# The gate operands of a PEER layer laid out by pairs of tokens

## The chip, the cores and the metric

The kernel runs on one core of a Trainium2 chip. The metric is the device time of one execution in microseconds, taken as the median of several runs. An engine is one of TensorE (matmuls, in the profile PE, its weight loads PEld), VectorE (DVE), ScalarE (ACT), GpSimd (POOL) and the queues that issue DMAs, SP's and POOL's here.

## The reference, cut to what matters

One inference step of a two-layer decoder for 512 prompt tokens and 8 single sample tokens, model width 1024. Each layer ends with a PEER block, a mixture of 16384 tiny experts. For every token and each of 8 heads it picks 16 experts, 128 in all, by two top-16 searches over 128 keys each; an expert's index is `i * 128 + j` of the two keys found. A gate `g` is the softmax of the 16 scores of a head.

```python
eidx = ...                       # (T, 8, 16): 128 * i + j
g = jax.nn.softmax(top_s, axis=-1)
u = u_tab[eidx]; vv = v_tab[eidx]
act = jax.nn.gelu(jnp.einsum('thkd,td->thk', u, h))
return jnp.einsum('thk,thkd->td', g * act, vv)
```

Written densely, the block is `y[t] = sum over i, j of G[t, i, j] * gelu(u[i, j] . h[t]) * v[i, j]`, where `G[t, i, j]` is the gate of expert (i, j) for token t, and zero for an expert that t did not pick.

## The kernel before, in words

Two of the four tiles of 128 prompt tokens in a layer are computed by gathering each token's experts: one indirect DMA on POOL and one pass over 1024 elements on VectorE for each of the rows of `u` and of `v` (`peer_tile`, lines 708 to 721). The other two tiles, 256 tokens, are computed densely in `dense_peer`, the function around the change. The gathers of a layer run beside its dense part; a planner puts VectorE's instructions on gathered rows between the dense ones, tied to marks that the dense code leaves (`tick`, line 104).

The dense part goes over the first key index i in 4 groups q of `QI` = 32. For a group there are three kinds of work:
- `acts(q)` (line 478): for each of the 32 values of i, a tile of `u` for 128 experts comes by DMA, is multiplied with the 256 tokens on TensorE (`ps_a`, 8 matmuls of 256 columns in group 0 and 24 in the others), and ScalarE writes `gelu` of it into `W[q]`, laid out (j, i, token).
- `gates(q)` (line 502): multiplies `W[q]` by the gates. This is what the change touches.
- the `y` matmuls (lines 570 to 574): for each i, `W[q][:, i]` times a tile of `v`, four matmuls of 512 columns (12 in most of the last group), added up in four PSUM banks over all 128 values of i.

While the `y` matmuls of group q run, the loop (lines 550 to 584) steps `acts(q + 1)` in the first 4 values of i and `gates(q + 1)` in the other 28. `acts(1)` is stepped beside `gates(0)`.

`gates(q)` makes the 128 by 32 matrix of gates of each token with two matmuls. Partition p of the operands is one of the token's 128 picks. The weights are a one-hot of the pick's j (128 columns, `oh[:, :, k]`); the moving operand is a one-hot of its i within the group times its gate (32 columns, `gi[:, c, :, t - t0]`), once for each of two 16-bit parts c of the gate, which are added in PSUM. The 32 result columns go to `ps[:, :, t - t1]`, a PSUM tile laid out (i, 16 tokens), so they are 64 bytes apart there; VectorE multiplies that tile into `W[q]` (line 537).

Two operands feed it:
- `gi`, for 32 tokens at a time: VectorE compares `sq`, the picks' i less 32 q, with `iotaJ`, a table of 128 values with each one standing 8 times (line 509), and multiplies the result by either part of the gate (line 514). Before the change `gi` is laid out (part, i, token): the 32 columns of a token are 32 elements of 2 bytes, 64 bytes, apart. The comparison runs over rows of 8 tokens.
- `oh`, for 8 tokens at a time, four buffers: VectorE compares in one instruction (line 521), and then the 128 columns of one token are 16 bytes apart; or ScalarE builds it with eight instructions and one over all (lines 527 and 530), and then they lie one behind the other. The choice (line 520) gives VectorE half of group 0 in both layers, and half of groups 1 to 3 in layer 1; all the rest is ScalarE's. There are 4 x 256 x 2 x 2 = 4096 gate matmuls and 256 one-hot operands.

The sample tokens have a PEER path of their own; in its top-16 pick, line 443 multiplies 256 elements of 2 bytes, of which one operand is read in rows of a single element (for the prompt tiles, in rows of 8).

The order of instructions on each engine is set by a planner from priorities and estimated durations.

Of the kernel before, what the change touches and what calls it, by code (L numbers as in the profile page):

```python
# [11 lines left out]
HF = mybir.dt.float16  # L12
# [3 lines left out]
OP = mybir.AluOpType  # L16
# [19 lines left out]
def body(ctx: ExitStack, tc: tile.TileContext, a):  # L36
    nc = tc.nc
    V, SC, PE, GP, SY = nc.vector, nc.scalar, nc.tensor, nc.gpsimd, nc.sync
# [27 lines left out]
    iotaJ = per.tile([128, 128, 8], HF, name="iotaJ")  # L66
# [37 lines left out]
    def tick(ins, k=1):  # L104
        if cur[0] is not None:
            anchors[cur[0]].extend([ins.ins.name] * k)
# [362 lines left out]
    def dense_peer(layer, dpa, open_rest, open_odd, smp):  # L469
# [3 lines left out]
        NQ, QI, NV = 4, 32, 4  # L473
# [28 lines left out]
        def gates(q):  # L502

            selJ, selb = dd["sel"]
            sq = dpb.tile([128, 256], HF, name="selq", tag="selq", bufs=1)
            V.tensor_scalar(sq, selb[:, 0, :], float(-q * QI), None, op0=OP.add)
            for t0 in range(0, 256, 32):
                gi = dpb.tile([128, 2, QI, 32], HF, name="gi", tag="gi", bufs=2)
                V.tensor_tensor(gi[:, 1].rearrange("p i (m w) -> p i m w", w=8),
                                sq[:, None, t0:t0 + 32].rearrange("p i (m w) -> p i m w", w=8)  # L510
                                .to_broadcast([128, QI, 4, 8]),
                                iotaJ[:, :QI, None, :].to_broadcast([128, QI, 4, 8]), op=OP.is_equal)
                for k in range(2):
                    V.tensor_tensor(gi[:, k], gi[:, 1], selb[:, 2 + k, None, t0:t0 + 32].to_broadcast([128, QI, 32]),  # L514
                                    op=OP.mult)
                for t1 in range(t0, t0 + 32, 16):
                    ps = pt.tile([128, QI, 16], F32, name="ps_g", tag="tr")
                    for t2 in range(t1, t1 + 16, 8):
                        oh = dpb.tile([128, 128, 8], HF, name="ohj", tag="ohj", bufs=4)
                        if (t2 // 8) % 4 < ([2, 2][layer] if not q else 2 * J_DVE[layer][q]):  # L520
                            V.tensor_tensor(oh, selb[:, 1, None, t2:t2 + 8].to_broadcast([128, 128, 8]), iotaJ,
                                            op=OP.is_equal)
                        else:

                            oh = oh.rearrange("p j k -> p (j k)").rearrange("p (k j) -> p j k", k=8)
                            for k in range(8):
                                SC.activation(oh[:, :, k], iota128, AF.Abs, scale=-1.0,  # L527
                                              bias=selJ[:, t2 + k:t2 + k + 1])
                            oh2 = oh.rearrange("p j k -> p k j")
                            SC.activation(oh2, oh2, AF.Relu, bias=1.0, scale=-1.0)  # L530
                        for k in range(8):
                            t = t2 + k
                            for c in range(2):
                                PE.matmul(ps[:, :, t - t1], oh[:, :, k], gi[:, c, :, t - t0], start=c == 0,  # L534
                                          stop=c == 1)
                    wv = W[q][:, :, t1:t1 + 16]
                    tick(V.tensor_tensor(wv, ps, wv, op=OP.mult), [3, 1][layer] if q else [5, 3][layer])  # L537
                    yield
# [4 lines left out]
        dpb, py = open_rest()  # L543
# [3 lines left out]
        for _ in gates(0):  # L547
            for _ in range(2):
                next(na, None)
        for q in range(NQ):  # L550
            na, ng = (na if not q else acts(q + 1), gates(q + 1)) if q + 1 < NQ else (iter(()), iter(()))
            for il in range(QI):
                i = q * QI + il
                w = W[q][:, il, :]
# [649 lines left out]
```

## Time and profile before

| | us |
|---|---|
| median of 3 runs | 3308.31 |
| lowest and highest | 3303.71, 3317.15 |
| the profiled execution | 3307.97 |
| its span, first to last instruction | 3306.3 |
| TensorE matmuls busy | 3051.4 |
| VectorE busy | 2426.3 |
| ScalarE busy | 1380.7 |
| GpSimd busy | 1340.0 |
| gate matmuls (line 534) busy | 265.5 in 4096 |
| gate weight loads (line 534) busy | 250.3 in 4096 |
| y matmuls (line 574) busy | 701.8 in 1536 |
| gate operands (lines 509 and 514) busy | 43.5 in 64, 87.4 in 128 |

Busy time counts every moment once, so matmuls that overlap in the pipeline add up to less than their number times their mean. Layer 0's gates run from 735 to 1518 us, layer 1's from 2444 to 3187 us.

### The profile page before, as it was taken

The page shows a single profiled execution, that of the slowest core. Times are in us where ns is not written, and L with a number is a line of the kernel's source. Part 1 is how long each engine was busy: PE and PEld are TensorE (multiplying, and loading weights), DVE is VectorE, ACT ScalarE, POOL GpSimd, SP SyncE. Part 2 cuts the span into 40 slices and gives each one's busy share as a digit, 9 for nine tenths or more (in the row PEclk, how much of TensorE's full clock was granted, in tenths as well). Part 3 has the DMA queues.
Part 4 walks back from the last instruction along what each step waited for, and adds up shares of the span by engine and source line. Part 5 has one row for each costly group of instructions (what it writes and reads, how often), then busy time and mean ns, then how long its engine had stood idle before and what let it go on. Part 6 is the DMA issues. An engine that isn't in the chain of part 4 may idle for free.

```text
span 3306.3 us, 50069 instructions
## 1 busy us (share of the span) xinstructions
PE 3051.4 (92%) x18048; PEld 2304.3 (70%) x18048; DVE 2426.3 (73%) x5093; ACT 1380.7 (42%) x3154; POOL 1340.0 (41%) x1061
## 2 busy tenths in 40 slices
PE   7998979859999999999998998789799999999999
PEld 7898646759757866866887643455689658768757
DVE  1489789999876668676425689869978776786775
ACT  2344021216666277386453234321246443353534
POOL 0046663564554436441000556534234454344340
PEclk9999989879999999999999988799899999999999
DMA  7788987888998989985655989867778999889885
GB/s 253 228 287 307 338 311 272 317 313 293 345 356 322 353 306 357 359 318 184 206 168 174 366 315 344 287 243 276 268 264 285 343 352 359 319 300 359 308 293 165
DMA packets 271563, 976.54 MB, mean 295 GB/s; under 512 B 30938, under 2 KB 31770, under 8 KB 271306
## 3 DMA queue, kind: packets, MB, share of 16 engines
q0 software_dynamic: 152064, 553.72, 46.5%
q1 hardware_dynamic: 119250, 419.62, 36.2%
q8 instruction: 142, 2.33, 0.3%
q14 instruction: 107, 0.88, 0.1%
HBM read 966.76 MB, written 6.46 MB: 294 GB/s over the span
## 4 chain that ended last, share of the span: by engine, by line
PE 66%; DVE 13%; DMA 9%; issue 5%; ACT 4%; POOL 3%; SPq 0%; DVEq 0%; POOLq 0%; ACTq 0%
PE y L574 19%; PE ps_d L231 7%; PE ps_g L534 7%; PE ps_a L488 6%; PE ps_a L489 5%; PE ps_a L491 5%; PE ps_a L494 3%; DMA gath<-peer_u,ix 3%; DMA gath<-peer_v,ix 3%; POOL gath L704 3%; DVE gath L713 2%; DVE x L720 2%; PE y L570 2%; PE y L571 2%; PE y L572 2%
## 5 line engine op out<-in xcount | busy, mean ns | idle before, releaser
L704 POOL DMA_INDIRECT gath<-peer_u,ix x512 | 649.0, 1268 | 1098.0 <-DVE ix L672 491.9
L704 POOL DMA_INDIRECT gath<-peer_v,ix x512 | 652.2, 1274 | 715.0 <-DVE x L720 383.9
L574 PE MATMUL y<-vb,W 128*128 128x512 f32 x1536 | 701.8, 602 | 1.2 <-DVE W L537 0.9
L720 DVE SCALAR_TENSOR_TENSOR x<-gath,act,x 128x1024 f32<-128x1024 f32 x512 | 655.5, 1280 | 64.4 <-DMA gath<-peer_v,ix 58.6
L713 DVE SCALAR_TENSOR_TENSOR gath<-gath,h_g 128x1024 f32<-128x1024 f32 x512 | 615.0, 1219 | 87.4 <-DMA gath<-peer_u,ix 83.6
L527 ACT ACTIVATE ohj<-iota,selJ 128x128 f16<-128x128 f32 x1408 | 425.8, 388 | 219.0 <-PE ps_g L534 205.7
L574 PEld LDWEIGHTS y<-vb,W 128*128 128x128 f32 x1536 | 282.7, 193 | 297.7 <-issue 293.7
L231 PE MATMUL ps_d<-hT,wt 128*128 128x128 f32 (+3 forms) x2048 | 430.7, 368 | 25.3 <-DMA wt<-peer_wq 5.8
L488 PE MATMUL ps_a<-hPh,wh 128*128 128x256 f32 x1536 | 403.7, 299 | 12.6 <-ACT wh L209 12.6
L231 PEld LDWEIGHTS ps_d<-hT,wt 128*128 128x128 f32 x2048 | 303.9, 198 | 137.8 <-issue 17.0
L489 PE MATMUL ps_a<-hPl,wh 128*128 128x256 f32 x1536 | 385.0, 287 | 0.0
L211 DVE TENSOR_TENSOR wl<-ub,wh 128x1024 fp32r<-128x1024 f32 x192 | 234.6, 1223 | 175.4 <-ACT wh L209 136.8
L209 ACT ACTIVATE wh<-ub 128x1024 fp32r<-128x1024 f32 x192 | 202.2, 1054 | 299.8 <-PE ps_a L489 251.6
L488 PEld LDWEIGHTS ps_a<-hPh,wh 128*128 128x128 f32 x1536 | 300.4, 196 | 26.5 <-ACT wh L209 14.6
L489 PEld LDWEIGHTS ps_a<-hPl,wh 128*128 128x128 f32 x1536 | 300.2, 195 | 10.1 <-issue 10.1
L534 PEld LDWEIGHTS <-ohj 128*128 128x128 f16 x4096 | 250.3, 130 | 72.1 <-issue 48.4
L534 PE MATMUL ps_g<-gi,ohj 128*128 128x32 f16 x4096 | 265.5, 234 | 18.9 <-DVE gi L514 11.6
L494 PE MATMUL ps_a<-hT,ub 128*128 128x256 f32 x1024 | 233.8, 390 | 31.4 <-ACT W L499 31.4
L494 PEld LDWEIGHTS ps_a<-hT,ub 128*128 128x128 f32 x1024 | 199.9, 197 | 61.8 <-ACT W L499 32.2
L499 ACT ACTIVATE W<-ps_a 128x256 f32<-128x256 f32 x256 | 96.2, 379 | 339.2 <-PE ps_a L491 149.3
L491 PE MATMUL ps_a<-hPh,wl 128*128 128x256 f32 x1536 | 225.1, 290 | 1.6 <-DVE wl L211 1.6
L491 PEld LDWEIGHTS ps_a<-hPh,wl 128*128 128x128 f32 x1536 | 200.2, 193 | 11.2 <-issue 8.4
(298 smaller groups left out, 3815.7 us busy)
## 6 DMA issues: line engine op xcount, KB each, us to landing
ub<-peer_ut SPq DMA_DIRECT2D x256, 512.0 KB
vb<-peer_v SPq DMA_DIRECT2D x256, 512.0 KB
wt<-w_in SPq DMA_DIRECT2D x64, 512.0 KB
wt<-peer_wq SPq DMA_DIRECT2D x64, 512.0 KB
wt<-w_out SPq DMA_DIRECT2D x32, 512.0 KB
gath<-peer_u,ix POOLq DMA_INDIRECT x512
gath<-peer_v,ix POOLq DMA_INDIRECT x512
wt<-w_k SPq DMA_DIRECT2D x16, 512.0 KB
```

Of the source, the lines that this page charges most:

```text
L211: tick(V.tensor_tensor(wl, w, wh.bitcast(F32), op=OP.subtract), k)
L231: z = PE.matmul(ps[:, :n], wt[:, c, :], rhs[:, c0 + c, :n], start=c0 + c == 0, stop=c0 + c == nk - 1)
L488: PE.matmul(ps, uh[:, c, :], hP[0][:, c, :], start=c == 0, stop=False)
L489: PE.matmul(ps, uh[:, c, :], hP[1][:, c, :], start=False, stop=False)
L491: PE.matmul(ps, ul[:, c, :], hP[0][:, c, :], start=False, stop=c == 7)
L494: z = PE.matmul(ps, u[:, c, :], hT[:, c, :256], start=c == 0, stop=c == 7)
L527: SC.activation(oh[:, :, k], iota128, AF.Abs, scale=-1.0, bias=selJ[:, t2 + k:t2 + k + 1])
L534: PE.matmul(ps[:, :, t - t1], oh[:, :, k], gi[:, c, :, t - t0], start=c == 0, stop=c == 1)
L574: PE.matmul(y[t][hf], w[:, ts], v[:, hs], start=i == 0, stop=i == 127)
L704: GP.indirect_dma_start(out=t, out_offset=None, in_=table, in_offset=bass.IndirectOffsetOnAxis(ap=ix[:, k:k + 1], axis=0))
L713: z = V.scalar_tensor_tensor(u, u, 1.0, h, op0=OP.mult, op1=OP.mult, accum_out=act[:, k:k + 1])
L720: z = V.scalar_tensor_tensor(x[t], v, act[:, k:k + 1], x[t], op0=OP.mult, op1=OP.add)
```

## The change

`gi` is laid out (part, pair of tokens, i, token of the pair) in place of (part, i, token). The 32 columns of one token's moving operand are then 2 elements, 4 bytes, apart, and the two tokens of a pair lie side by side. The three VectorE instructions that fill it for 32 tokens go over the same 1024 elements in that order, and read the three sources through one view each: pairs of tokens, each pair repeated for the 32 values of i. `iotaJ` is read two of its eight equal elements at a time. Everything else stays.

```diff
--- before.py
+++ after.py
@@ -505,14 +505,13 @@
             sq = dpb.tile([128, 256], HF, name="selq", tag="selq", bufs=1)
             V.tensor_scalar(sq, selb[:, 0, :], float(-q * QI), None, op0=OP.add)
             for t0 in range(0, 256, 32):
-                gi = dpb.tile([128, 2, QI, 32], HF, name="gi", tag="gi", bufs=2)
-                V.tensor_tensor(gi[:, 1].rearrange("p i (m w) -> p i m w", w=8),
-                                sq[:, None, t0:t0 + 32].rearrange("p i (m w) -> p i m w", w=8)
-                                .to_broadcast([128, QI, 4, 8]),
-                                iotaJ[:, :QI, None, :].to_broadcast([128, QI, 4, 8]), op=OP.is_equal)
+
+                gi = dpb.tile([128, 2, 16, QI, 2], HF, name="gi", tag="gi", bufs=2)
+                sv = [z[:, t0:t0 + 32].rearrange("p (m w) -> p m w", w=2)[:, :, None, :].to_broadcast([128, 16, QI, 2])
+                      for z in (sq, selb[:, 2], selb[:, 3])]
+                V.tensor_tensor(gi[:, 1], sv[0], iotaJ[:, None, :QI, :2].to_broadcast([128, 16, QI, 2]), op=OP.is_equal)
                 for k in range(2):
-                    V.tensor_tensor(gi[:, k], gi[:, 1], selb[:, 2 + k, None, t0:t0 + 32].to_broadcast([128, QI, 32]),
-                                    op=OP.mult)
+                    V.tensor_tensor(gi[:, k], gi[:, 1], sv[1 + k], op=OP.mult)
                 for t1 in range(t0, t0 + 32, 16):
                     ps = pt.tile([128, QI, 16], F32, name="ps_g", tag="tr")
                     for t2 in range(t1, t1 + 16, 8):
@@ -531,7 +530,7 @@
                         for k in range(8):
                             t = t2 + k
                             for c in range(2):
-                                PE.matmul(ps[:, :, t - t1], oh[:, :, k], gi[:, c, :, t - t0], start=c == 0,
+                                PE.matmul(ps[:, :, t - t1], oh[:, :, k], gi[:, c, (t - t0) // 2, :, t % 2], start=c == 0,
                                           stop=c == 1)
                     wv = W[q][:, :, t1:t1 + 16]
                     tick(V.tensor_tensor(wv, ps, wv, op=OP.mult), [3, 1][layer] if q else [5, 3][layer])
```

## Rows read from the trace of the kernel before

**Rows 1.** The page: busy time by engine; the chain that ended last, by line.
```profile
PE 3051.4 (92%) x18048; PEld 2304.3 (70%) x18048; DVE 2426.3 (73%) x5093; ACT 1380.7 (42%) x3154; POOL 1340.0 (41%) x1061
...
PE y L574 19%; PE ps_d L231 7%; PE ps_g L534 7%; PE ps_a L488 6%; PE ps_a L489 5%; PE ps_a L491 5%; PE ps_a L494 3%; DMA gath<-peer_u,ix 3%; DMA gath<-peer_v,ix 3%; POOL gath L704 3%; DVE gath L713 2%; DVE x L720 2%; PE y L570 2%; PE y L571 2%; PE y L572 2%
```

**Rows 2.** Busy time by engine in seven stretches; columns named by their first line.
```profile
core 0: us, PE busy (x) PEld busy (x) DVE busy (x) ACT busy (x) POOL busy (x), PEclk, DMA share, GB/s
735.00:875.00 140.00, 130.49 (x1253) 125.81 (x1254) 127.65 (x171) 93.37 (x211) 72.92 (x52) 0.95 0.87 303
890.00:1040.00 150.00, 149.64 (x839) 85.71 (x840) 99.81 (x158) 103.66 (x282) 78.60 (x68) 0.95 0.94 353
1182.00:1289.00 107.00, 104.69 (x717) 64.81 (x715) 79.13 (x113) 100.74 (x280) 53.16 (x44) 0.98 0.87 312
1418.00:1519.00 101.00, 95.46 (x674) 57.90 (x673) 72.32 (x99) 95.70 (x260) 43.88 (x35) 0.97 0.81 289
2444.00:2578.00 134.00, 128.49 (x1243) 123.38 (x1243) 113.90 (x144) 89.54 (x198) 53.72 (x38) 0.96 0.75 261
2594.00:2738.00 144.00, 143.02 (x816) 82.43 (x816) 109.52 (x176) 50.55 (x140) 79.46 (x68) 0.99 0.96 357
2875.00:2962.00 87.00, 87.00 (x647) 54.98 (x646) 71.81 (x105) 50.36 (x135) 39.73 (x31) 1.00 0.85 295
```

**Rows 3.** Instructions on one-hot operands: duration ns min/median/max, first and last start.
```profile
L534 PE MATMUL ps_g<-gi,ohj x4096: 216/234/272, 735.1 to 3186.6; 128*128 128x32 f16 x196
...
L527 ACT ACTIVATE ohj<-iota,selJ x1408: 383/387/404, 710.6 to 3176.2; 128x128 f16<-128x128 f32 x176
...
L521 DVE TENSOR_TENSOR ohj<-selb,iotaJ x80: 670/683/694, 729.5 to 3168.3; 128x1024 f16<-128x1024 f16 x80
```

**Rows 4.** TensorE in order of time from 1249.85 us: start, duration, instruction, count.
```profile
1249.85 3.80 PE L534 MATMUL ps_g<-gi,ohj 128*128 128x32 f16 x64
```

**Rows 5.** TensorE in order of time, 1281.35 to 1284.77 us, granted clock 0.50.
```profile
1281.52 1.08 PE L534 MATMUL ps_g<-gi,ohj 128*128 128x32 f16 x16 [2.22 <-ACT ohj L530]
...
1283.19 0.41 PE L489 MATMUL ps_a<-hPl,wh 128*128 128x256 f32 x1
...
1283.41 0.41 PE L488 MATMUL ps_a<-hPh,wh 128*128 128x256 f32 x1
```

**Rows 6.** TensorE in order of time from 2872.3 us, granted clock 1.00.
```profile
2872.12 0.28 PE L488 MATMUL ps_a<-hPh,wh 128*128 128x256 f32 x1
2872.24 0.28 PE L489 MATMUL ps_a<-hPl,wh 128*128 128x256 f32 x1
```

**Rows 7.** TensorE from 1249.85 us, cut after two and after three gate matmuls.
```profile
1249.85 0.27 PE L534 MATMUL ps_g<-gi,ohj 128*128 128x32 f16 x2
...
1249.85 0.33 PE L534 MATMUL ps_g<-gi,ohj 128*128 128x32 f16 x3
```

**Rows 8.** Weight loads ahead of a near and a far row; 29 far matmuls.
```profile
1249.42 0.10 PEld L534 LDWEIGHTS <-ohj 128*128 128x128 f16 x1 [0.24 <-issue]
...
2885.17 0.14 PEld L534 LDWEIGHTS <-ohj 128*128 128x128 f16 x1 [0.24 <-issue]
...
2885.59 1.91 PE L534 MATMUL ps_g<-gi,ohj 128*128 128x32 f16 x29
```

**Rows 9.** Waits, 1182 to 1289 us: us in total, times, longest.
```profile
ACT ohj L527 <- PE ps_g L534: 6.3, 4, 3.3
...
PEld L534 <- ACT ohj L530: 3.8, 5, 2.4
...
PE ps_g L534 <- ACT ohj L530: 2.2, 1, 2.2
```

**Rows 10.** Groups by line and shape: count, busy us, mean ns, idle before.
```profile
L509 DVE TENSOR_TENSOR gi<-selq,iotaJ 128x1024 f16<-128x1024 f16 x64 | 43.5, 681 | 0.0
...
L514 DVE TENSOR_TENSOR gi<-gi,selb 128x1024 f16<-128x1024 f16 x128 | 87.4, 685 | 0.6
...
L211 DVE TENSOR_TENSOR wl<-ub,wh 128x1024 fp32r<-128x1024 f32 x192 | 234.6, 1223 | 175.4 <-ACT wh L209 136.8 <-issue 25.8 <-ACT W L499 4.8
...
L446 DVE TENSOR_TENSOR oh<-oh 128x256 f16<-128x256 f16 x16 | 4.5, 282 | 0.2
```

**Rows 11.** VectorE in order of time from 2422 us, the sample tokens.
```profile
2422.49 0.41 DVE L443 TENSOR_TENSOR oh<-oh,tmp 64x256 f16<-64x256 f16 x1
```

## The prediction

> **What bounds the kernel now.** I read the page first, then the stretches in which gate matmuls run, then single matmuls. On the page TensorE is busy 92% of the span and the gate matmuls stand on the chain that ended last with 7% of it, some 231 us of 3306.3 [rows 1]: the reader is to see that there is time of this line to win, and that it is not the largest line. The second view cuts out the stretches in which gates run, one for each of four groups of 32 rows of W in each of two layers [rows 2]. The reader is to look at which engine fills a stretch. In groups 1 and 2 of layer 1 (the last two rows; group 3, from 3102 us on, is like group 2) TensorE is busy 143.0 of 144 and 87.0 of 87 us while ScalarE has 51 and 50: TensorE alone sets the pace. Group 1 of layer 0 (second row) is alike, 149.6 of 150 with ScalarE at 103.7. In groups 2 and 3 of layer 0 ScalarE, which builds all one-hot operands there, is busy 100.7 of 107 and 95.7 of 101 us, about as much as TensorE. In the two groups 0 the chain changes hands: TensorE 130.5 of 140 and 128.5 of 134, VectorE 127.7 and 113.9.
>
> The third view counts the work [rows 3]: 4096 gate matmuls, each with its own weight load of 128 columns. Of the 256 one-hot operands, each serving 16 matmuls, ScalarE builds 1408 / 8 = 176 with their 128 weight columns lying one behind the other (2816 matmuls, "near" below) and VectorE 80 with weight columns 16 bytes apart (1280 matmuls, "far").
>
> **What one gate matmul costs, and why.** 64 near matmuls in a row take 3.80 us [rows 4]; less the 0.234 us of the last one [rows 3], that is 3.57 / 63 = 0.057 us from start to start. [...]
>
> [...] The first matmuls of a row speak on this [rows 7]. Two last 0.27, three 0.33: with 0.234 for the last, the second starts 0.04 after the first and the third 0.06 after the second. A pair can be issued in 0.04; the longer step begins where a matmul is behind another that streams. The weights speak too [rows 8]: the first load of a near row takes 0.10 us, of a far row 0.14, so 128 columns at a pitch of 16 bytes cost 0.04 more to fetch; and the far rows run at (1.91 - 0.234) / 28 = 0.060. If the weight load set the near pace, 0.04 more on it would make the far pace about 0.10. It is 0.060, so the near pace is not the load's. What is left is the moving operand, 32 columns at a pitch of 64 bytes, or the output, 32 PSUM columns at a pitch of 64 bytes. The change closes the first to 4 bytes and leaves the second as it is.
>
> [...]
>
> **The change part by part.** *Near gate matmuls:* 2816, now 0.057. [...] I take 0.040, the one step between gate matmuls in the trace with no other before the first, because there the weight load and the issue are counted in. Saved: 0.017 each, 47.9 us in all before anything else gets in the way.
>
> *Far gate matmuls:* 1280, now 0.060. The load at 16 bytes stays, and I hold that it now sets their pace: saved 0. The other end, all falling to 0.040, is 25.6 us.
>
> *Where the saving reaches the end.* Both dense parts end with TensorE's last y matmuls, and what follows waits for these, so time won where TensorE is the bound carries to the end. Groups 1 to 3 of layer 1, half near: 768 x 0.017 = 13.1 us, all of it. Group 1 of layer 0: 512 x 0.017 = 8.7, all. Groups 2 and 3 of layer 0: 1024 x 0.017 = 17.4, but ScalarE is idle only 6.3 and 5.3 us there [rows 2], waits for TensorE's release of a one-hot buffer only 6.3 us in group 2, and TensorE is already caught waiting for ScalarE, 2.2 us for a matmul and 3.8 for a load [rows 9]; I count half, 8.7. Late next is the one-hot operand of ScalarE. Groups 0: 2 x 256 x 0.017 = 8.7; the chain there passes through VectorE and ScalarE as well, half, 4.4. Sum 13.1 + 8.7 + 8.7 + 4.4 = 34.9 us.
>
> *VectorE's gate operands:* 192 operations before and after, on the same 1024 elements, now in rows of 2 where they were in rows of 8 and 32. Rows of 8 (L509) and of 32 (L514) both take 0.68 [rows 10], so row length has not mattered down to 8. Rows of one element do: 256 elements take 0.41 in L443, where the sample tokens leave it rows of one [rows 11], against 0.28 for 256 in one piece [rows 10]. Rows of two still hold a pair of 2-byte elements next to each other; I take 0.68 and a cost of 0. The far end is one element at a time, as in 1024 elements of 4 bytes, 1.223 [rows 10]: 192 x 0.54 = 104 us of VectorE. A gain is excluded, since a row of any kind has not gone below 0.68. Only the groups 0 have no room for it (VectorE idle 12.3 and 20.1 us there, and its order is fixed); 24 operations in each make 2 x 24 x 0.54 = 26 us. In the other groups VectorE is at 67 to 83% and hides it. [...]
>
> *What else moves:* no instruction, DMA, tile size or wait is added or taken; one-hot building, the multiply into W, and SP's and POOL's queues are untouched in number. The order of the program comes from a planner that prices instructions; should it price the new patterns otherwise, it may order some work anew, which the trace of before cannot show. I leave that to the range. The DMA engines are busy 0.75 to 0.96 of these stretches [rows 2]; a stretch that gets shorter by 6 us in 100 would bring the fullest to the brim, which is one more reason to count groups by half where another engine is near; I charge 0 beyond that.
>
> The sum is made against the profiled execution, 3307.97 us (0.34 under the median shown): 3307.97 - 34.9 = 3273.
>
> **The rivals.**
> A. *The pace stays*, because PSUM's strided output or the handing over from load to matmul sets it: 3308. For: every gate matmul has the same output pitch, so no row separates output from input; also groups 2 and 3 of layer 0 could give less than half. Against: the price of a pitch on the weight side in [rows 8].
> B. *More is won*: near pace 0.030, far pace 0.040, 2816 x 0.027 + 1280 x 0.020 = 102 us, of which the share above (34.9 of 47.9) reaches the end, 74: 3234. [...] Against: the 0.14 load of far rows.
> C. *VectorE takes the groups 0*: rows of two run one element at a time and the matmul's pace stays. Price 26 us: 3334. It decides from 0.683 + 16.5 / 48 = 1.03 us for an operation on, and only if the matmuls give nothing; if they give 34.9, the two together end at 3299. For: VectorE is at 91% in group 0 of layer 0, and L443's rows of one. Against: L509 already reads iotaJ in short rows at the full rate.
>
> **How the numbers follow.** Forecast 0.47, A 0.31, B 0.10, C 0.12. The likeliest gives 3273, by itself 3253 to 3291. About 0.5%, 16.5 us, is what a measurement of this kernel can tell from no change; forecast and B lie beyond it on the fast side, 0.57; A within it, 0.31; C beyond it on the slow side, 0.12. The range runs from 3245, which leaves out half of B, to 3318, which takes in A with its scatter and leaves out C.
>
> **What would show it.** Right: a row of 64 near matmuls in about 2.8 us instead of 3.80; far rows still near 0.060; L509's and L514's successors at 0.68; layer 1's groups 1 to 3 shorter by some 4 us each, layer 0's groups 2 and 3 with more TensorE waits on the one-hot operand of ScalarE. Wrong: 64 near matmuls still in 3.8 us (A), far rows falling with the near ones (B), or gate operands above 1 us (C).

## The result and the profile after

The changed kernel takes 3260.17 us (median of 4 runs, 3255.13 to 3263.07) where the kernel before takes 3311.49 (4 runs, 3303.71 to 3317.15): a ratio of 0.9839, 95% interval 0.9818 to 0.9861, some 51 us won. The forecast was 3273 with a range of 3245 to 3318. The profiled execution of the changed kernel takes 3263.07 us with a span of 3261.4, so 44.9 us less span than before; the accounts below are made of these two spans. Every engine runs the same instructions in the same order in both traces (on VectorE one neighbouring pair has changed places); only the gate operands lie differently, and lines behind L514 have moved up by one (the gate matmul is now L533, ScalarE's one-hot L526 and L529, VectorE's L520, the multiply into W L536; the comparison is L512).

The page of the changed kernel answers to [rows 1]: busy time by engine and the chain that ended last.

```profile
PE 2977.0 (91%) x18048; PEld 2228.5 (68%) x18048; DVE 2450.0 (75%) x5093; ACT 1379.5 (42%) x3154; POOL 1369.9 (42%) x1061
...
PE y L573 13%; PE ps_d L231 7%; POOL gath L703 6%; DMA gath<-peer_u,ix 4%; PE ps_a L488 4%; PE ps_a L489 4%; PE ps_a L491 4%; DMA gath<-peer_v,ix 4%; PE ps_g L533 3%; PE ps_a L494 2%; DVE gath L712 2%; ACT ohj L526 2%; DVE x L719 2%; PE y L569 2%; PE y L570 2%
```

TensorE is busy 74 us less, VectorE 24 us more, and the gate matmuls' part of the chain has gone from 7% to 3%. Where VectorE's 24 us come from is seen in the instructions on the gate operands (duration in ns min/median/max, first and last start), which answer to [rows 3]:

```profile
L533 PE MATMUL ps_g<-gi,ohj x4096: 189/193/288, 741.2 to 3142.1; 128*128 128x32 f16 x196
L514 DVE TENSOR_TENSOR gi<-gi,selb x128: 672/686/702, 740.4 to 3123.8; 128x1024 f16<-128x1024 f16 x128
L512 DVE TENSOR_TENSOR gi<-selq,iotaJ x64: 1044/1081/1147, 737.2 to 3119.9; 128x1024 f16<-128x1024 f16 x64
```

The two multiplies L514 stay at 0.686, the comparison L512 went from 0.681 [rows 10] to 1.081: 64 x 0.400 = 25.6 us more for VectorE.

TensorE in order of time (start, duration, instruction, count, and in brackets an idle time before it): a near row at the full clock, a pair alone, a row at the low clock, a far row; and, by engine as in [rows 2], the stretch of the row at the low clock.

```profile
1230.60 2.03 PE L533 MATMUL ps_g<-gi,ohj 128*128 128x32 f16 x64
...
1398.38 0.23 PE L533 MATMUL ps_g<-gi,ohj 128*128 128x32 f16 x2
...
1494.03 1.03 PE L533 MATMUL ps_g<-gi,ohj 128*128 128x32 f16 x16 [1.63 <-ACT ohj L529]
...
2883.70 1.68 PE L533 MATMUL ps_g<-gi,ohj 128*128 128x32 f16 x25
...
1489.00:1495.10 6.10, 3.10 (x48) 2.63 (x48) 1.93 (x4) 5.15 (x11) 0.00 (x0) 0.50 0.00 0
```

Less 0.193 for the last one, 64 near matmuls now start (2.03 - 0.193) / 63 = 0.029 us apart, where it was 0.057 [rows 4]. The far ones are where they were, (1.68 - 0.193) / 24 = 0.062. The row of 1494 stands in a stretch of granted clock 0.50: its last matmul takes 0.242 in the trace, so it runs at (1.03 - 0.242) / 15 = 0.053. Before, the clock made no difference: (1.08 - 0.234) / 15 = 0.056 at 0.50 [rows 5] and 0.057 at 1.00 [rows 4], while matmuls of 256 columns start 0.21 apart at 0.50 [rows 5] and 0.12 at 1.00 [rows 6]; so it was not the clock that set the 0.057. Now it makes nearly a factor of two, 0.053 against 0.029; the first experiment shows that this comes with the output's pitch.

The stretches in which gates run, by engine as in [rows 2] (us, then busy time of PE, PEld, DVE, ACT, POOL, the granted clock, DMA share, GB/s):

```profile
741.00:876.00 135.00, 124.34 (x1252) 119.54 (x1253) 129.26 (x170) 92.50 (x208) 77.02 (x51) 0.95 0.88 309
892.00:1025.00 133.00, 131.53 (x842) 70.81 (x842) 101.96 (x157) 101.05 (x277) 80.37 (x68) 1.00 1.00 392
1167.00:1268.00 101.00, 93.21 (x711) 51.88 (x709) 81.48 (x112) 99.47 (x277) 58.37 (x44) 0.97 0.90 328
1398.00:1495.00 97.00, 84.86 (x671) 46.31 (x669) 73.62 (x98) 95.49 (x259) 44.30 (x35) 0.95 0.84 299
2570.00:2706.00 136.00, 134.67 (x814) 75.20 (x814) 111.09 (x172) 49.56 (x137) 81.53 (x67) 1.00 0.98 373
2843.00:2923.00 80.00, 80.00 (x650) 48.29 (x648) 74.08 (x104) 49.48 (x131) 39.57 (x30) 1.00 0.91 316
```

Layer 1 (last two rows) is still TensorE's own, though in group 1 of either layer (second and fifth row) the DMA engines are now busy 1.00 and 0.98 of the time. In groups 2 and 3 of layer 0 (third and fourth row) it is no longer: ScalarE is busy 99.47 of 101 and 95.49 of 97 us, TensorE 93.21 and 84.86. The waits of group 2 say the same (waiter and what it waits for: us in total, times, longest), against 3.8, 2.2 and 6.3 in [rows 9]:

```profile
PEld L533 <- ACT ohj L529: 10.5, 10, 2.8
...
PE ps_g L533 <- ACT ohj L529: 6.9, 6, 2.6
ACT ohj L526 <- PE ps_g L533: 1.5, 2, 1.0
```

TensorE now waits for ScalarE's operand, and ScalarE hardly ever for TensorE.

**Where the time went.** From the first to the last gate matmul of each group, in us; the fourth and fifth columns are the prediction's terms as it had them (0.017 a near matmul) and the same terms with the 0.028 that was measured.

| group | before | after | won | term | term at 0.028 |
|---|---|---|---|---|---|
| layer 0, group 0 | 138.7 | 133.8 | 4.9 | 2.2 | 3.6 |
| layer 0, group 1 | 149.4 | 132.1 | 17.3 | 8.7 | 14.3 |
| layer 0, group 2 | 105.3 | 100.0 | 5.3 | 4.4 | 7.2 |
| layer 0, group 3 | 99.1 | 96.5 | 2.6 | 4.4 | 7.2 |
| layer 1, group 0 | 132.3 | 126.0 | 6.3 | 2.2 | 3.6 |
| layer 1, group 1 | 142.6 | 135.8 | 6.8 | 4.4 | 7.2 |
| layer 1, group 2 | 85.7 | 79.1 | 6.6 | 4.4 | 7.2 |
| layer 1, group 3 | 84.1 | 77.5 | 6.6 | 4.4 | 7.2 |
| sum | | | 56.4 | 34.9 | 57.3 |

The sums of the terms are of the terms before rounding, 34.9 is the prediction's own.

TensorE was given 2816 x 0.028 = 78.8 us; 56.4 of them shortened the gate groups. Outside the groups 11.5 us went the other way: the first gate came 6.1 us later (735.1 to 741.2), the front of layer 1 (last y matmul of layer 0 to the first W matmul of layer 1) took 690.1 instead of 685.4, and 0.7 elsewhere.

One profile of each kernel does not settle these shares. The changed kernel was profiled once more beside the later kernels (3283.49 us, on another chip): there the gate groups are 40.3 us shorter than before, not 56.4, at the same pace of 0.029, and 15.8 us go the other way outside them. Its group 1 of layer 1, by engine:

```profile
2584.70:2725.00 140.30, 136.10 (x814) 75.73 (x814) 112.28 (x174) 49.58 (x137) 81.65 (x67) 0.99 0.97 364
```

That group takes 140.1 us there instead of 135.8, and TensorE is idle for 4 of them.

### The profile page after: what moved, and what is told of

Same layout as the page of the kernel before. It is cut to its first block, busy times and chain, and to the rows that moved or that the text cites. A ratio compares the mean times of both kernels' runs of the same rounds, so it can differ in the third digit from the quotient of the medians.

```text
span 3261.4 us, 50069 instructions
## 1 busy us (share of the span) xinstructions
PE 2977.0 (91%) x18048; PEld 2228.5 (68%) x18048; DVE 2450.0 (75%) x5093; ACT 1379.5 (42%) x3154; POOL 1369.9 (42%) x1061
## 4 chain that ended last, share of the span: by engine, by line
PE 53%; DVE 13%; DMA 11%; issue 11%; POOL 6%; ACT 5%; SPq 0%; POOLq 0%; DVEq 0%; ACTq 0%
PE y L573 13%; PE ps_d L231 7%; POOL gath L703 6%; DMA gath<-peer_u,ix 4%; PE ps_a L488 4%; PE ps_a L489 4%; PE ps_a L491 4%; DMA gath<-peer_v,ix 4%; PE ps_g L533 3%; PE ps_a L494 2%; DVE gath L712 2%; ACT ohj L526 2%; DVE x L719 2%; PE y L569 2%; PE y L570 2%
## 5 line engine op out<-in xcount | busy, mean ns | idle before, releaser
L703 POOL DMA_INDIRECT gath<-peer_u,ix x512 | 664.8, 1298 | 1077.6 <-DVE ix L671 490.5
L703 POOL DMA_INDIRECT gath<-peer_v,ix x512 | 666.5, 1302 | 669.9 <-DVE x L719 355.3
L719 DVE SCALAR_TENSOR_TENSOR x<-gath,act,x 128x1024 f32<-128x1024 f32 x512 | 655.7, 1281 | 72.4 <-DMA gath<-peer_v,ix 66.9
L526 ACT ACTIVATE ohj<-iota,selJ 128x128 f16<-128x128 f32 x1408 | 425.7, 390 | 174.3 <-PE ps_g L533 174.1
L533 PEld LDWEIGHTS <-ohj 128*128 128x128 f16 x4096 | 180.7, 121 | 86.9 <-issue 46.5
L533 PE MATMUL ps_g<-gi,ohj 128*128 128x32 f16 x4096 | 190.4, 204 | 33.6 <-ACT ohj L529 19.0
```

The costliest lines, as they stand in the source:

```text
L526: SC.activation(oh[:, :, k], iota128, AF.Abs, scale=-1.0, bias=selJ[:, t2 + k:t2 + k + 1])
L533: PE.matmul(ps[:, :, t - t1], oh[:, :, k], gi[:, c, (t - t0) // 2, :, t % 2], start=c == 0, stop=c == 1)
L703: GP.indirect_dma_start(out=t, out_offset=None, in_=table, in_offset=bass.IndirectOffsetOnAxis(ap=ix[:, k:k + 1], axis=0))
L719: z = V.scalar_tensor_tensor(x[t], v, act[:, k:k + 1], x[t], op0=OP.mult, op1=OP.add)
```

## The experiments

The runs came in three groups, each on one chip with the kernel before beside it. The four of the first group, on the pitches of output and moving columns, ran once each (before: 3328.58 us there); the others were timed in five rounds (before: 3323.92, and 3320.83 for the last two kernels), and their ratios are to these.

### Was the output's pitch a part of the 0.057?

Before and after, the 32 output columns of a gate matmul lie 64 bytes apart in PSUM. In two kernels, made from before and from after, they lie side by side, and the multiply into W reads them at a pitch of 128 bytes instead:

```
-ps = pt.tile([128, QI, 16], F32, name="ps_g", tag="tr")
+ps = pt.tile([128, 16, QI], F32, name="ps_g", tag="tr")
...
-PE.matmul(ps[:, :, t - t1], oh[:, :, k], ...
+PE.matmul(ps[:, t - t1, :], oh[:, :, k], ...
...
-tick(V.tensor_tensor(wv, ps, wv, op=OP.mult), ...
+tick(V.tensor_tensor(wv, ps.rearrange("p t i -> p i t"), wv, op=OP.mult), ...
```

> The kernel before, with the gate matmul's 32 output columns side by side in PSUM (they were 64 bytes apart) and the moving columns still 64 bytes apart. Theory M (the moving operand's pitch sets the near pace): near rows stay at 0.057 us from start to start, 64 of them in 3.8 us, and the time stays within 0.5% of 3311. Rival P (PSUM's strided output sets it too): near rows fall well under 0.050, toward the 0.029 of the changed kernel.

> The changed kernel, with the output columns side by side in PSUM as well. Theory M with the output free: near rows stay at 0.029, far rows at 0.060. Rival P: the near rows' 0.029 still holds a part of the output's pitch and falls further, to 0.025 or less.

TensorE in order of time, a row of 64 in the one made from before:

```profile
1258.94 3.80 PE L534 MATMUL ps_g<-gi,ohj 128*128 128x32 f16 x64
```

and in the one made from after, with a row of 16 at the low clock and, by engine, its stretch:

```profile
1233.63 1.75 PE L533 MATMUL ps_g<-gi,ohj 128*128 128x32 f16 x64
...
1496.81 0.61 PE L533 MATMUL ps_g<-gi,ohj 128*128 128x32 f16 x16 [2.05 <-ACT ohj L529]
...
1488.70:1497.40 8.70, 2.42 (x64) 2.02 (x64) 4.42 (x9) 8.22 (x19) 0.00 (x0) 0.50 0.11 46
```

From before, 64 take 3.80 us as they did [rows 4], and the time is 3330.55: the output's pitch held nothing while the moving operand was read at 64 bytes. From after, they take 1.75, less 0.176 for the last one 0.025 apart: now the output's pitch is worth 0.004. That holds at the full clock. At the low one, 0.50, the last 16 of layer 0 take 0.61 us where the changed kernel took 1.03: less 0.188 for its last matmul they are 0.028 apart, against 0.053. There the output's pitch makes nearly a factor of two, and without it the clock makes little difference (0.025 and 0.028). In the trace of the changed kernel 74 of the 4096 gate matmuls start at the low clock. The kernel made from after takes 3267.93. The multiply into W, which reads the other way round, stayed at 0.691 us in the first and 0.686 in the second. Rival A is out, and what it named, the strided output, returns as the next limit behind the moving operand: 0.029 with it, 0.025 without.

### Which pitch of the moving columns counts?

The operands laid out by 4 and by 8 tokens, so that moving columns lie 8 and 16 bytes apart. The edit is that of the change with another width:

```
-gi = dpb.tile([128, 2, 16, QI, 2], HF, name="gi", tag="gi", bufs=2)
+gi = dpb.tile([128, 2, 8, QI, 4], HF, name="gi", tag="gi", bufs=2)
...
-PE.matmul(ps[:, :, t - t1], oh[:, :, k], gi[:, c, (t - t0) // 2, :, t % 2], ...
+PE.matmul(ps[:, :, t - t1], oh[:, :, k], gi[:, c, (t - t0) // 4, :, t % 4], ...
```

> The changed kernel laid out by four tokens, so that the moving columns are 8 bytes apart and VectorE goes over rows of 4. Theory M with a limit between 4 and 16 bytes: near rows at 0.029 if two columns in 16 bytes are enough, between 0.029 and 0.057 if the cost grows with the pitch. The comparison that reads the table of indices: if the table's pitch of 16 bytes between rows costs by the row, 0.53 us of reading plus half of the extra 0.40 us, so 0.85 to 0.90; if only rows of two are slow, 0.68.

> The changed kernel laid out by eight tokens, so that the moving columns are 16 bytes apart and VectorE goes over rows of 8. [...] Rival (the pitch of 64 bytes was special, a matter of its power of two): near rows stay at 0.029.

A near row of 64 at 8 bytes, and the comparison there:

```profile
1229.91 2.21 PE L533 MATMUL ps_g<-gi,ohj 128*128 128x32 f16 x64
...
L512 DVE TENSOR_TENSOR gi<-selq,iotaJ x64: 671/681/689, 734.0 to 3139.7; 128x1024 f16<-128x1024 f16 x64
```

and at 16 bytes:

```profile
1251.59 4.00 PE L533 MATMUL ps_g<-gi,ohj 128*128 128x32 f16 x64
```

The near pace is 0.029 at 4 bytes, (2.21 - 0.198) / 63 = 0.032 at 8, (4.00 - 0.240) / 63 = 0.060 at 16, and 0.057 at 64. The step lies between 8 and 16 bytes: two columns in 16 bytes run at 0.032, one at 0.060. The times are 3283.37 and 3335.34 us. At 16 bytes nothing is left of the gain, as its pace wants it. At a width of 4 tokens L512 reads 8 of every 16 bytes of its table (rows of 4), and it takes 0.681 again: the 0.85 to 0.90 expected if a pitch of 16 bytes cost by the row did not come (the 0.53 of reading in it is an estimate that [rows 10] give, 1024 x (0.681 - 0.282) / 768).

### What does the slow comparison cost, and what slows it?

The comparison reads its numbers i from a table in which each stands 8 times, a pair out of every 16 bytes. Theory: that pitch slows it; rival: the rows of two do. A table of its own, in which each number stands twice and the pairs lie one behind the other, keeps the rows of two:

```
+iotaP = per.tile([128, 32, 2], HF, name="iotaP")
+V.tensor_copy(iotaP, iota128[:, :32, None].to_broadcast([128, 32, 2]))
...
-V.tensor_tensor(gi[:, 1], sv[0], iotaJ[:, None, :QI, :2].to_broadcast([128, 16, QI, 2]), op=OP.is_equal)
+V.tensor_tensor(gi[:, 1], sv[0], iotaP[:, None, :QI, :].to_broadcast([128, 16, QI, 2]), op=OP.is_equal)
```

It was timed beside the changed kernel itself.

> The changed kernel itself, timed beside the three that follow. 3260, 0.984 of the kernel before.

> The changed kernel with a table of indices in which each value stands twice and the pairs lie one behind the other (32 x 2 elements), for the comparison that took 1.08 us with pairs 16 bytes apart. Theory T (the table's pitch is what costs): the comparison at 0.68 us, VectorE 64 x 0.40 = 26 us less busy, and since VectorE sets the pace in the two groups 0 alone, 16 x 0.40 = 6 us or less off the time: 3253 to 3260. Rival R (rows of two are slow by themselves): the comparison stays at 1.08 and the time at 3260.

```profile
L514 DVE TENSOR_TENSOR gi<-selq,iotaP x64: 670/681/726, 733.5 to 3131.1; 128x1024 f16<-128x1024 f16 x64
```

The comparison (here L514) is back at 0.681 with rows of two, so rows of two are not slow by themselves; and rows of four at the same pitch of 16 bytes were not slow either. Slow, at 1.081, were rows of two that stand alone in 16 bytes. The time does not show it: 3273.88 us (4 runs), ratio 0.9858 (0.9835 to 0.9882), beside 3277.79 and 0.9857 (0.9831 to 0.9882) of the changed kernel. Nor do the two groups 0, where 6 us or less were expected: they take 134.2 and 126.8 us, and 133.8 and 126.0 in the changed kernel. So most of the 25.6 us of VectorE were hidden; the intervals leave room for a few us.

### Does the far pace hang on the weights' pitch?

VectorE's one-hot operands, 128 weight columns 16 bytes apart in after, are built by pairs of tokens, so that weight columns lie 4 bytes apart too (on top of the table above, widened to 128 numbers; the old table, which only the searches still read, is cut to 16):

```
...
-V.tensor_tensor(oh, selb[:, 1, None, t2:t2 + 8].to_broadcast([128, 128, 8]), iotaJ, op=OP.is_equal)
+oh = oh.rearrange("p j k -> p (j k)").rearrange("p (m j w) -> p m j w", m=4, w=2)
+V.tensor_tensor(oh, selb[:, 1, t2:t2 + 8].rearrange("p (m w) -> p m w", w=2)[:, :, None, :]
+                .to_broadcast([128, 4, 128, 2]),
+                iotaP[:, None, :, :].to_broadcast([128, 4, 128, 2]), op=OP.is_equal)
+ohk = [oh[:, k // 2, :, k % 2] for k in range(8)]
...
-PE.matmul(ps[:, :, t - t1], oh[:, :, k], ...
+PE.matmul(ps[:, :, t - t1], ohk[k], ...
...
```

> As the one before, and the one-hot weights that VectorE builds are laid out by pairs of tokens too, so that their 128 columns lie 4 bytes apart (they were 16). Theory W (the weights' pitch sets the far pace): far rows fall from 0.060 to 0.029, building one stays at 0.68 us. Saved 1280 x 0.031 = 40 us, of which groups 1 to 3 of layer 1 carry 768 x 0.031 = 24 to the end and the groups 0 half of theirs: 3220 to 3235. Rival: far rows stay near 0.060 because an operand built by VectorE comes with something else that is slow; then 3255.

TensorE in order of time, a row with far matmuls; the building of the operand; group 2 of layer 0 by engine and its waits:

```profile
2882.18 1.42 PE L539 MATMUL ps_g<-gi,ohj 128*128 128x32 f16 x43
...
L523 DVE TENSOR_TENSOR ohj<-selb,iotaP x80: 669/682/718, 730.2 to 3114.2; 128x1024 f16<-128x1024 f16 x80
...
1156.00:1257.00 101.00, 92.97 (x706) 51.49 (x704) 76.79 (x110) 99.05 (x276) 52.74 (x42) 0.97 0.88 320
...
PEld L539 <- ACT ohj L534: 10.3, 7, 2.8
```

All gate matmuls now start (1.42 - 0.193) / 42 = 0.029 apart, and building costs the same 0.682. The time is 3246.08 us, ratio 0.9773 (0.9753 to 0.9792), 28 us under the kernel with the new table, where 20 to 35 under it were expected. So it was the weights' pitch of 16 bytes that held the far pace at 0.060; the load ahead of this row takes 0.10 us, where that of a far row took 0.14 [rows 8]. Groups 2 and 3 of layer 0 have no far matmuls and take 100.4 and 96.5 us, as in the changed kernel (100.0 and 96.5).

### Is ScalarE the bound of layer 0's groups 2 and 3?

There VectorE takes over half of the one-hot operands, as in layer 1 (on top of the kernel just told of):

```
-J_DVE = [[1, 0, 0, 0], [1, 1, 1, 1]]
+J_DVE = [[1, 0, 1, 1], [1, 1, 1, 1]]
```

> As the one before, with VectorE building half of the one-hot weights in groups 2 and 3 of layer 0 too, where ScalarE built all. Theory S (ScalarE sets the pace there, so that those two groups gave 8 of the 29 us that their matmuls became shorter): groups 2 and 3 of layer 0 get shorter by some 20 us together, 3200 to 3215. Rival (those groups lost their gain to the DMA engines or to VectorE): VectorE gets 32 x 0.68 = 22 us more there and they stay as long or grow, 3225 or more.

Group 2 of layer 0 by engine and its waits:

```profile
1155.00:1235.00 80.00, 79.03 (x662) 42.68 (x661) 73.77 (x107) 51.47 (x137) 42.09 (x32) 1.00 0.91 327
...
ACT ohj L531 <- PE ps_g L539: 23.1, 10, 8.1
...
PEld L539 <- ACT ohj L534: 1.3, 2, 1.1
```

ScalarE falls from 99.05 of 101 us to 51.47 of 80, TensorE fills the stretch again, and it is ScalarE that waits now. The groups take 79.4 and 72.4 us instead of 100.4 and 96.5: 45.1 us shorter. Some of that is work that moved: fewer of TensorE's instructions stand in the stretch (662 instead of 706), and from group 2 to group 3 it is 147.1 us instead of 134.5. Less these 12.6, 32.5 us are won; the time is 3213.06 us, ratio 0.9677 (0.9655 to 0.9700), 33 us under the last one. ScalarE was the bound, and what the change gave TensorE there mostly stood behind it.

### Both together, and all operands by VectorE

The side-by-side output put on the kernel just told of, and then VectorE building every one-hot operand in groups 1 to 3:

```
-J_DVE = [[1, 0, 1, 1], [1, 1, 1, 1]]
+J_DVE = [[2, 2, 2, 2], [2, 2, 2, 2]]
```

> e5_split with the gate output lying side by side in PSUM (token-major), the multiply into W reading it at a pitch of 128 bytes. Theory P (the output's pitch is now what holds the pace): near and far matmuls both at 0.025 us where e5_split has 0.029; 4096 x 0.004 = 16 us of TensorE saved at most, about 8 to 12 us of time, some 3200 to 3205 beside 3213. Rival Q (the pace no longer reaches the end, since building the operands and the front of layer 1 set the gate stretches): the pace falls all the same and the time stays within 5 us of e5_split.

> e6_out with all one-hot operands of groups 1 to 3 of both layers built by VectorE: 80 more operations of 0.683 us for VectorE (55 us), 640 fewer of 0.387 and 80 fewer of 1.04 for ScalarE. Theory S (ScalarE, where it builds, still holds up gates): L0 g1 shorter by a few us, the other groups alike, time below e6_out by 3 to 10 us. Rival V (VectorE, at 67 to 83% in these groups, is the bound as soon as it builds them all): the groups grow, time above e6_out by 5 us or more.

Gate matmuls with the output side by side (all of the kernel, then one row), and group 2 of layer 0:

```profile
L539 PE MATMUL ps_g<-gi,ohj x4096: 176/176/207, 738.1 to 3098.4; 128*128 128x32 f16 x196
...
1157.53 1.75 PE L539 MATMUL ps_g<-gi,ohj 128*128 128x32 f16 x64
...
1157.00:1235.00 78.00, 76.83 (x659) 40.44 (x657) 74.00 (x106) 51.60 (x137) 45.41 (x31) 1.00 0.91 334
```

The same group with all operands built by VectorE:

```profile
1153.00:1247.00 94.00, 90.00 (x665) 45.57 (x662) 86.55 (x125) 0.68 (x2) 59.80 (x36) 0.96 0.86 308
```

The pace falls to 0.025 for all gate matmuls, and the eight groups together are 804.6 us long instead of 812.4, but the time, 3208.93 us, ratio 0.9674 (0.9649 to 0.9698), can't be told from the 0.9677 without this edit: nearer to rival Q than to P, but the two intervals, some 8 us either way each, do not exclude P's 8 to 12 us. With all operands on VectorE (224 built there instead of 112, so 112 more and not the 80 that the expectation counts) the time is 3217.41, ratio 0.9689 (0.9665 to 0.9714), also not to be told apart. The groups grow as rival V has it (layer 0's group 2 from 77.6 to 94.5, VectorE busy 86.55 of 94), but the program's order shifts with this edit (from group 2 to group 3 of layer 0 it is 133.4 us instead of 147.1, and from the last gate to the last y matmul 94.0 instead of 114.6), so that the runs do not separate VectorE's load from the new order. No version timed here is shown to be faster than the split of layer 0 with pairs on both sides.

### What was given back in the front of layer 1

The front of layer 1 has no gate matmul, and its work is the same in all kernels. It was not always as long. From the last y matmul of layer 0 to layer 1's first W matmul, by engine, in the kernel before:

```profile
1610.80:2296.20 685.40, 600.76 (x2839) 405.27 (x2838) 478.37 (x1386) 231.10 (x592) 255.63 (x208) 0.90 0.76 266
```

in the changed kernel:

```profile
1588.10:2278.20 690.10, 599.90 (x2838) 401.63 (x2837) 478.18 (x1391) 231.55 (x592) 260.88 (x208) 0.90 0.76 264
```

with moving columns 16 bytes apart:

```profile
1613.60:2323.70 710.10, 617.98 (x2838) 409.50 (x2836) 482.77 (x1406) 231.16 (x593) 264.24 (x211) 0.88 0.75 259
```

and with layer 0's operands split:

```profile
1547.10:2260.20 713.10, 623.64 (x2838) 410.43 (x2837) 478.49 (x1391) 230.22 (x592) 253.76 (x208) 0.87 0.74 255
```

The reader is to look at the third column from the end, the granted clock, and at TensorE's busy time: 600 us of TensorE at a granted clock of 0.90 become 618 and 624 for the same 2838 matmuls at 0.88 and 0.87, while VectorE, ScalarE and POOL have the same work. At 0.90 the front takes 682 to 692 us in six of the twelve profiles (the changed kernel has two), before and after among them; at 0.87 to 0.89 it takes 697 to 713 in the other six. So the front's length goes with the clock granted there; a profile is one execution, and that of the kernel with the operands split (3234.29 us) is the slowest of its five. What lowers the clock is not settled: the kernel with 16 bytes gained nothing elsewhere and has the low clock too, so "a faster gate part costs clock later" is not shown. For before and after the clock is 0.90 in both, and their 4.7 us lie within the 682 to 692 that kernels of that clock show.

## Why the prediction was right, and where its sizes were off

The mechanism was right: the moving operand at 64 bytes set the near pace (0.057, and 0.029 at 4 bytes), the weights at 16 bytes the far pace (0.060, and 0.029 at 4 bytes), and TensorE's saving reached the end where TensorE is the bound. Two errors of size lay on opposite sides.

- **The near pace.** The step that was mis-sized is "I take 0.040, the one step between gate matmuls in the trace with no other before the first". It measured 0.029, so the saving was 0.028 each and 78.8 us in all, not 47.9. The step from the first to the second matmul is no floor: the pair that stands alone at 1398.38 us of the changed kernel lasts 0.23, so that even there the second starts 0.23 - 0.193 = 0.037 after the first, while rows of 64 run at 0.029. In the row behind it, from 1399.48 us on, the first step is 0.038 and the next ones 0.029: the first step is longer than the steady one.
- **The far pace.** "I hold that it now sets their pace: saved 0": right, 0.060 to 0.061, and the pairs on the weight side show the cause. Rival B's near pace came (0.029 against its 0.030), its far pace did not.
- **The shares.** With 0.028 in the terms the sum is 57.3, and the groups lost 56.4. That they meet within 1 us is in part luck: in the second profile of the same kernel the groups lost 40.3. Layer 1's groups 1 to 3 gave 20.0 of 21.5, but 14.6 in the second profile, where group 1 gave 2.5 and TensorE did not fill it (136.10 of 140.30 us, with the DMA engines, which the prediction charged nothing, busy 0.97 of the time); whether they hold it is not tested. "I count half" was too much for layer 0's groups 2 and 3, 7.9 of a possible 28.7, because ScalarE's 6 us of slack were used up at once, and too little for the groups 0, 11.2 of 14.3. Group 1 of layer 0 gave 17.3, more than its 14.3; its granted clock was 1.00 after and 0.95 before [rows 2]. In the second profile it gave 13.4 at a clock of 0.99, so the clock alone does not explain the difference.
- **VectorE.** "I take 0.68 and a cost of 0" was wrong for the comparison, 1.081 (a sign of rival C), and right for the cost as far as the time can tell. It erred by looking at the rows and not at the table's pitch: L509 read full 16 bytes of it, L512 reads 4. 16 of the 64 slow ones stand in the groups 0, 6.4 us, and with them gone the groups 0 are as long as with them. Rows of two took 0.681 on the dense table and 1.081 in L512 of the changed kernel.
- **What was not in the sum.** 11.5 us outside the gate groups. The 4.6 of them between layer 0's first W matmul and its first gate (181.8 to 186.4) did not come again: 184.0 in the second profile of the same kernel and 181.2 to 183.6 in the kernels built on it. They lie within the scatter of single profiles, and so do the front's 4.7.

So the profiled 3263.07 instead of 3273 is +22.4 us of gain from the pace, -0.9 from the shares and -11.5 from outside: the time came out nearer to the forecast than the pace did, because part of the larger gain was given back elsewhere. Rival A is refuted by the side-by-side output; rival C had its sign, 1.081, in one of three operations, and the matmuls' gain was far above its price.

## What to carry to other kernels

Read a TensorE operand's pitch as well as its size: with the 2-byte columns here the pace was 0.029 and 0.032 with moving columns 4 and 8 bytes apart and 0.060 with 16, and 0.029 with weight columns 4 bytes apart and 0.060 with 16 (8 was not tried there); pairs were close enough on both sides, and the side that builds them kept rows of two, at 0.68 us for 1024 elements. Compare a pace at both granted clocks: here 0.057 and 0.056 went with a slow moving operand, 0.029 and 0.053 with a strided output, 0.025 and 0.028 with neither. And follow a saving to the engine next in line before counting on it: here ScalarE held back nearly three quarters of it in two of the eight groups, and one line that moved its work to VectorE won another 33 us.

## What the runs showed of the hardware that was not expected

- 32 moving columns with a weight load of their own can run 0.025 us apart when all three operands are dense enough; at the full clock a strided output costs 0.004 more, at the low one 0.053 against 0.028, and behind a moving operand at 64 bytes nothing (64 take 3.80 us either way).
- 16 bytes between moving columns is no better than 64: 0.060 against 0.057.
- VectorE pays for a pitch too: 1024 elements of 2 bytes, of which one source is read in pairs out of every 16 bytes, take 1.081 us instead of 0.681; read in fours out of every 16 bytes they take 0.681.
